# First stage in rounds of one k-tile, and matmul operands at one place modulo 512 bytes

## The chip, the core and the metric

The kernel runs on one core of one Trainium2 chip. The metric is device time in microseconds (us) of one execution; several runs are taken and the median is given. The core's engines are TensorE (PE in the profile; its weight loads stand apart as PEld), VectorE (DVE), ScalarE (ACT), GpSimd (POOL) and SyncE (SP), which here only issues DMAs. Each engine runs its own instructions in order and waits on semaphores for the others.

## What is computed

Two layers of a hybrid encoder on 256 tokens of width 1024, all in float32. Cut to what matters here:

```python
cond = jax.nn.silu(c)
for l in range(2):
    mod = (cond @ ada_w[l] + ada_b[l])[:, None, :]          # 1024 -> 6 x 1024
    sh1, sc1, g1, sh2, sc2, g2 = jnp.split(mod, 6, axis=-1)
    h = rmsnorm(x, norm1_g[l]) * (1 + sc1) + sh1
    proj = h @ w_in[l] + b_in[l]                            # 1024 -> 6733 columns
    ...                                                     # three attention mixers on parts of proj
    x = x + g1 * (y @ w_out[l])                             # y: gated sum of three branch projections
    h = rmsnorm(x, norm2_g[l]) * (1 + sc2) + sh2
    gu = h @ w_ffn_in[l]                                    # 1024 -> 2 x 2816
    x = x + g2 * ((silu(gu[..., :2816]) * gu[..., 2816:]) @ w_ffn_out[l])
return rmsnorm(x, final_g)
```

Almost all of the time goes into the dense products: `w_in`, `w_branch`, `w_out`, `w_ffn_in`, `w_ffn_out`.

## The kernel before, in words

**Splitting.** Each float32 operand of a dense product is split into a high part (rounded to the fp32r type by ScalarE) and a low part (the rest, by a VectorE subtraction). A product is then three matmuls: high·high, high·low, low·high (`mm3`, lines 322 to 324, with the weights' columns as the moving operand; `mm3_T`, lines 466 to 468, with the activations as the moving operand). `block_W` (lines 499 and 500) puts high and low activations side by side: one matmul of 512 columns and one of 256.

**Tiles.** The contraction dimension is cut into k-tiles of 128. The split activations lie in one tile `hT` (high and low, two token halves, eight k-tiles); the feed-forward's hidden activations in `aT0` and `aT1`. Weights arrive by DMA in raw tiles of up to four k-tiles, are split into a pair of tiles `whi` and `wlo` of up to two k-tiles (a piece), and the pieces wait in a pool: six in `splitp`, and a few more in an extra pool that exists in the first stage (`start`, 2), around the output projection (4) and in `ffn_out` (`end0`, `end1`, 3). `new_piece` takes from `splitp` first and from the extra pool when `splitp` is full.

**Places.** Pools are laid out in SBUF one behind the other, in the order in which they are opened, and tiles in a pool likewise, so a tile's address follows from the sizes ahead of it. Counted as bytes past a multiple of 512, in the kernel before: `hT` starts at 256; the pieces of `splitp` at 128; the pieces of the extra pools, `aT0` and `aT1` at 352; the attention outputs `oh` and `ol` at 416 (layer 0) and 480 (layer 1). A block of 128 fp32 columns is 512 bytes, so all slices of `hT`, `aT` and the 512-column weights start at the same remainder as their tile. A block of 456, 326 or 320 columns starts its second k-tile elsewhere.

**The first stage** (`start`, lines 1082 to 1243) works the first four blocks of `w_in` of layer 0 (512, 456, 512 and 512 columns). It needs, for each k-tile, two sums of the adaLN product (`ada_sum`, line 348, on VectorE, which read a raw `ada_w` tile of 1 MB), the modulated and split activations (`modulate`, lines 1144 to 1149), and the split weights (`split`, lines 1159 and 1162). Before, it runs in four rounds of two k-tiles: a raw weight tile `raw0` holds two k-tiles, ten of them are allowed (`START_RAWS`), and a piece holds two k-tiles. In the first round each piece is split in two halves, with the halves of the two k-tiles interleaved. The order of VectorE, ScalarE, TensorE and GpSimd in this stage is the order in which the code is written. The list `plan` sets the order of all loads on SyncE's queue; eight completion lanes are used in turn by the loads of SyncE and ScalarE, so a load waits until the eighth one before it has landed. After the stage the pieces are made by `pump` and taken by `get`.

Of the kernel before, what the change touches and what calls it, by code (L numbers as in the profile page):

```python
# [11 lines left out]
F32 = mybir.dt.float32  # L12
# [6 lines left out]
P = 128  # L19
# [75 lines left out]
def hybrid_encoder(ctx: ExitStack, tc: tile.TileContext, a):  # L95
# [4 lines left out]
    START_BLOCKS, START_RAWS, START_EXTRA = 4, 10, 2  # L100
# [49 lines left out]
    def emit_load(i):  # L150
        it = plan[i]
        if it[0] == "p":
            _, src, off, w = it
            raw = start_pool[0].tile([P, 2 * 512], F32, tag="raw0", name="raw0", bufs=START_RAWS)
            nc.sync.dma_start(raw[:, :2 * w], flat(src, off, [[4 * w, P], [1, 2 * w]]))
            raws[i] = raw
            return
        if it[0] == "w":
            _, src, off, nk, w = it
        else:  # L160
            src, nk, w = a["ada_w"], 4, 512
# [163 lines left out]

    hTT = const.tile([P, 2, T, KT, P], F32R, name="hT")
    hT = [hTT[:, i] for i in range(2)]
# [718 lines left out]
    def start_piece(i, p):  # L1046
        w = len(IN_BLOCKS[i][1])
        return ("p", a["w_in"], IN_OFF[i] + (p // 2) * P * 4 * w + (p % 2) * 2 * w, w)

    ada = ada_items(0, "s1")  # L1050
    for p in range(KT // 2):
        wp = [start_piece(i, p) for i in range(START_BLOCKS)]
        plan += [ada[2 * p], *wp, ada[1]] if p == 0 else [ada[2 * p], *wp[:-1], ada[2 * p + 1], wp[-1]]
# [28 lines left out]
    def start():  # L1082
# [50 lines left out]
        def sums(kt, between=lambda: None):  # L1133
            r = take()
            ada_sum(0, kt, 0, r)
            between()
            ada_sum(0, kt, 1, r)
            free(0)
# [12 lines left out]
        def split(n=1):  # L1151

            w = plan[st_item[0]][3]
            r = take()
            hi, lo = new_piece(2, w)
            cs = [slice(i * 2 * w // n, (i + 1) * 2 * w // n) for i in range(n)]

            def high(i):
                nc.scalar.activation(hi[:, cs[i]], r[:, cs[i]], AF.Copy)

            def low(i):
                nc.vector.tensor_sub(lo[:, cs[i]], r[:, cs[i]], hi[:, cs[i]].bitcast(F32))  # L1162
                if i == n - 1:
                    free(1)

            return high, low
# [5 lines left out]
        def products(i, kt, pc):  # L1172
            k = kt % 2
            if IN_BLOCKS[i][0] in BY_FEATURE:
                for f in range(len(IN_BLOCKS[i][1]) // P):
                    feature_mm(first[i], f, kt, k, pc)
            else:
                for t in range(T):
                    mm3(first[i][t], hT[0][:, t, kt, :], hT[1][:, t, kt, :], pc[0][:, k], pc[1][:, k],
                        start=kt == 0, stop=kt == KT - 1)  # L1180

        for p in range(KT // 2):
            k0 = 2 * p
            if p == 0:
                sums(0)
                parts = [split(2)]
                parts[0][0](0)
                rest = modulate(0, on_act=False)
                parts[0][1](0)
                rest()  # L1190
                for i in range(1, START_BLOCKS):
                    parts.append(split(2))
# [9 lines left out]
                for i, (high, low) in enumerate(parts):  # L1202
                    if i > 1:
                        high(1)
                    low(1)
                    if i == 0:
                        rest()
            else:
                sums(k0)
                high, low = split()  # L1210
                high(0)
                rest = modulate(k0)
                low(0)
                rest()
                for i in range(1, START_BLOCKS):
                    if i == START_BLOCKS - 1:
                        sums(k0 + 1)
                    high, low = split()
                    high(0)
                    if i == START_BLOCKS - 1:  # L1220
                        rest = modulate(k0 + 1)
                    low(0)
            pcs = [ready.pop(0) for _ in range(START_BLOCKS)]
            for i in range(START_BLOCKS):
                products(i, k0, pcs[i])
            if p:
                rest()
            for i in range(START_BLOCKS):
                products(i, k0 + 1, pcs[i])
            got[0] += 4  # L1230
            for pc in pcs:
                piece_out[pc[3]] -= 1
            if p == 0:
# [5 lines left out]
            if p == 1:  # L1239
# [13 lines left out]
    with tc.tile_pool(name="start", bufs=1) as start_pool[0]:  # L1253
        piece_pools[1] = (start_pool[0], START_EXTRA, 4 * START_BLOCKS)
# [89 lines left out]
```

## Time and profile before

| | us |
|---|---|
| median of 3 runs (lowest, highest) | 862.37 (862.35, 864.16) |
| the profiled execution, its own time | 861.53 |
| its span, from the first to the last instruction | 859.8 |
| TensorE busy in the span | 840.1 |
| VectorE busy in the span | 664.4 |
| ScalarE busy in the span | 496.1 |

The span is cut into stretches in one view, and into instructions in order of time in another. A matmul's end is modelled in this profile, and matmuls overlap in their pipeline, so a matmul's price is read from the distance between the starts of two consecutive ones, not from its duration. The granted clock of TensorE is 1.00 (2.4 GHz) in the stretches shown below.

### The profile page before, as it was taken

What the parts mean: (1) busy time and instruction counts of PE and PEld (TensorE: products, weight loads), DVE (VectorE), ACT (ScalarE), POOL (GpSimd) and SP (SyncE); (2) the same over time, 40 slices, a digit from 0 to 9 for tenths busy, and PEclk for the clock granted to TensorE, in tenths of its full rate; (3) what the DMA queues carried; (4) which work ended last, traced back from release to release, by engine and by line L of the source; (5) the groups of instructions that cost most, each with busy time, mean ns of one, the idle gap of its engine ahead of it and who ended that gap; (6) DMA issues with size and microseconds to landing.
All of it is one profiled execution on the core that took longest, in us unless ns stands there. A gap on an engine that the chain in (4) does not pass through costs nothing.

```text
span 859.8 us, 14019 instructions
## 1 busy us (share of the span) xinstructions
PE 840.1 (98%) x5366; PEld 752.3 (87%) x5366; DVE 664.4 (77%) x1148; ACT 496.1 (58%) x874; POOL 73.9 (9%) x131
## 2 busy tenths in 40 slices
PE   6999999999999999999999999999999999999996
PEld 5899898999888888888889999898998888888885
DVE  5996988969896888797475886787998766768734
ACT  6566956764564656564355576767466545556521
POOL 5720210000010000000012013000000100000001
PEclk9999999999999999999999999999999999999998
DMA  9977566669846756599354456387795565546701
GB/s 350 416 263 241 196 218 229 221 245 335 327 151 245 282 215 244 219 342 380 120 195 127 156 189 233 148 282 267 281 373 184 200 223 223 192 150 255 311 23 50
DMA packets 32707, 199.91 MB, mean 233 GB/s; under 512 B 4040, under 2 KB 4304, under 8 KB 14208
## 3 DMA queue, kind: packets, MB, share of 16 engines
q1 hardware_dynamic: 30816, 194.25, 61.1%
q0 software_dynamic: 1232, 4.31, 1.6%
q8 instruction: 42, 0.69, 0.3%
q10 hardware_dynamic: 592, 0.46, 0.2%
q14 instruction: 25, 0.20, 0.1%
HBM read 197.96 MB, written 1.05 MB: 231 GB/s over the span
## 4 chain that ended last, share of the span: by engine, by line
PE 86%; DVE 6%; DMA 3%; issue 2%; ACT 2%; ACTq 0%; POOLq 0%; POOL 0%; DVEq 0%
PE ps_g L499 15%; PE ps_g L322 11%; PE ps_g L324 11%; PE ps_g L323 11%; PE ps_g L500 8%; PE ps_g L466 7%; PE ps_g L467 7%; PE ps_g L468 7%; DVE wlo L196 2%; DMA raw<-in_ada_w_dram 2%; DVE raw L348 2%; PE ps_x L692 1%; PE ps_x L834 1%; PE ps_x L690 1%; PE ps_x L827 1%
## 5 line engine op out<-in xcount | busy, mean ns | idle before, releaser
L196 DVE TENSOR_TENSOR wlo<-raw,whi 128x1024 fp32r<-128x1024 f32 (+5 forms) x284 | 313.1, 1122 | 78.3 <-ACT whi L195 76.2
L195 ACT ACTIVATE whi<-raw 128x1024 fp32r<-128x1024 f32 (+5 forms) x284 | 271.7, 971 | 164.3 <-PE ps_g L324 61.0
L499 PE MATMUL ps_g<-hT,whi 128*128 128x512 f32 x576 | 203.2, 394 | 0.0
L500 PE MATMUL ps_g<-hT,wlo 128*128 128x256 f32 x576 | 162.9, 283 | 0.0
L348 DVE CUSTOM_DVE_ANT_0 raw<-raw,cond,adab 128x1024 f32<-128x1024 f32 x96 | 123.1, 1299 | 24.1 <-DMA raw<-in_ada_w_dram 24.1
L466 PE MATMUL ps_g<-hT,whi 128*128 128x256 f32 x480 | 138.5, 289 | 0.0
L468 PE MATMUL ps_g<-hT,wlo 128*128 128x256 f32 x480 | 135.4, 282 | 0.0
L467 PE MATMUL ps_g<-hT,whi 128*128 128x256 f32 x480 | 135.3, 282 | 0.0
L499 PEld LDWEIGHTS ps_g<-hT,whi 128*128 128x128 f32 x576 | 108.2, 188 | 24.7
L322 PE MATMUL ps_g<-whi,hT 128*128 128x512 f32 (+4 forms) x320 | 118.5, 370 | 1.7 <-ACT hT L1148 1.7
L323 PE MATMUL ps_g<-wlo,hT 128*128 128x512 f32 (+4 forms) x320 | 116.5, 364 | 0.1
L324 PE MATMUL ps_g<-whi,hT 128*128 128x512 f32 (+4 forms) x320 | 116.5, 364 | 0.0
L500 PEld LDWEIGHTS ps_g<-hT,wlo 128*128 128x128 f32 x576 | 108.3, 188 | 0.1
L466 PEld LDWEIGHTS ps_g<-hT,whi 128*128 128x128 f32 x480 | 90.4, 188 | 3.7 <-issue 3.7
L467 PEld LDWEIGHTS ps_g<-hT,whi 128*128 128x128 f32 x480 | 90.5, 189 | 0.3 <-issue 0.3
L468 PEld LDWEIGHTS ps_g<-hT,wlo 128*128 128x128 f32 x480 | 90.4, 188 | 0.3 <-issue 0.3
L322 PEld LDWEIGHTS ps_g<-whi,hT 128*128 128x128 f32 x320 | 60.2, 188 | 11.9 <-ACT hT L1148 2.3
L324 PEld LDWEIGHTS ps_g<-whi,hT 128*128 128x128 f32 x320 | 60.1, 188 | 8.1 <-DVE hT L1149 0.3
L323 PEld LDWEIGHTS ps_g<-wlo,hT 128*128 128x128 f32 x320 | 60.3, 188 | 7.9 <-DVE wlo L1162 0.6
L322 PE MATMUL ps_g<-whi,aT 128*128 128x512 f32 (+1 forms) x176 | 67.0, 381 | 0.0
L323 PE MATMUL ps_g<-wlo,aT 128*128 128x512 f32 (+1 forms) x176 | 66.8, 380 | 0.0
L324 PE MATMUL ps_g<-whi,aT 128*128 128x512 f32 (+1 forms) x176 | 66.7, 379 | 0.0
(226 smaller groups left out, 1175.3 us busy)
## 6 DMA issues: line engine op xcount, KB each, us to landing
raw<-in_ada_w_dram SPq DMA_DIRECT2D x46, 1024.0 KB, 5.4
raw<-in_w_ffn_in_dram SPq DMA_DIRECT2D x40, 1024.0 KB, 4.8
raw<-in_w_in_dram SPq DMA_DIRECT2D x30, 1024.0 KB, 5.5
raw<-in_w_ffn_out_dram SPq DMA_DIRECT2D x20, 1024.0 KB, 5.2
raw<-in_w_branch_dram SPq DMA_DIRECT2D x12, 768.0 KB, 4.7
raw<-in_w_in_dram SPq DMA_DIRECT2D x16, 512.0 KB, 13.3
raw<-in_w_out_dram SPq DMA_DIRECT2D x8, 1024.0 KB, 7.2
raw<-in_w_in_dram SPq DMA_DIRECT2D x8, 768.0 KB, 4.4
```

The source lines that it names most:

```text
L195: nc.scalar.activation(hi, r, AF.Copy)
L196: nc.vector.tensor_sub(lo, r, hi.bitcast(F32))
L322: nc.tensor.matmul(ps, lh, wh, start=start, stop=False)
L323: nc.tensor.matmul(ps, lh, wl, start=False, stop=False)
L324: nc.tensor.matmul(ps, ll, wh, start=False, stop=stop)
L348: nc.vector.tensor_tensor_reduce(out=wj, in0=wj, in1=cond, op0=OP.mult, op1=OP.add, scale=ngain[:, l, int(name[2]) - 1, k:k + 1] if name[: ...
L466: nc.tensor.matmul(ps, wh[:, c], ah, start=first, stop=False, skip_group_check=True)
L467: nc.tensor.matmul(ps, wh[:, c], al, start=False, stop=False, skip_group_check=True)
L468: nc.tensor.matmul(ps, wl[:, c], ah, start=False, stop=stop, skip_group_check=True)
L499: nc.tensor.matmul(ps[f], pc[0][:, k, c], hTT[:, :, :, kt, :], start=kt == 0, stop=False)
L500: nc.tensor.matmul(ps[f][:, :S], pc[1][:, k, c], hT[0][:, :, kt, :], start=False, stop=kt == KT - 1)
L690: nc.tensor.matmul(p[:, 0:P], q[:, 0:P], k[:, 0:P], start=True, stop=True)
```

## The change

1. The first stage runs in eight rounds of one k-tile. A raw weight tile holds one k-tile, so a DMA is half as large, and twenty are allowed (the same room). A piece holds one k-tile. Per round the order is: the two sums, two high splits, the modulation, two low splits, the low part of the activations, the other two blocks' splits; then the products. A piece is given back as soon as its block's products are recorded. In the list of loads each `ada_w` tile is followed by the four weight tiles of its k-tile.
2. Three tiles that nothing uses (`gap0`, 384 bytes; `gap1`, 128 bytes; `gap2`, 288 bytes per partition) move what is allocated behind them. Counted past a multiple of 512 bytes, `hT`, all pieces, `aT0` and `aT1` now start at 128; `oh` and `ol` at 192 (layer 0) and 256 (layer 1).

```diff
-    START_BLOCKS, START_RAWS, START_EXTRA = 4, 10, 2
+    START_BLOCKS, START_RAWS, START_EXTRA = 4, 20, 2
...
-            raw = start_pool[0].tile([P, 2 * 512], F32, tag="raw0", name="raw0", bufs=START_RAWS)
-            nc.sync.dma_start(raw[:, :2 * w], flat(src, off, [[4 * w, P], [1, 2 * w]]))
+            raw = start_pool[0].tile([P, 512], F32, tag="raw0", name="raw0", bufs=START_RAWS)
+            nc.sync.dma_start(raw[:, :w], flat(src, off, [[4 * w, P], [1, w]]))
...
+    const.tile([P, 96], F32, name="gap0")
     hTT = const.tile([P, 2, T, KT, P], F32R, name="hT")
+    const.tile([P, 32], F32, name="gap1")
+    small.tile([P, 72], F32, name="gap2", bufs=1)
...
-    ada = ada_items(0, "s1")
-    for p in range(KT // 2):
-        wp = [start_piece(i, p) for i in range(START_BLOCKS)]
-        plan += [ada[2 * p], *wp, ada[1]] if p == 0 else [ada[2 * p], *wp[:-1], ada[2 * p + 1], wp[-1]]
+    for kt, unit in enumerate(ada_items(0, "s1")):
+        plan += [unit, *(start_piece(i, kt) for i in range(START_BLOCKS))]
...
-        for p in range(KT // 2):
-            k0 = 2 * p
-            if p == 0:
-                sums(0)
-                parts = [split(2)]
-                parts[0][0](0)
+        for kt in range(KT):
+            sums(kt)
+            if kt == 0:
+                low = split()
                 rest = modulate(0, on_act=False)
-                parts[0][1](0)
+                low()
                 rest()
                 for i in range(1, START_BLOCKS):
-                    parts.append(split(2))
-                    high, low = parts[i]
-                    high(0)
+                    low = split()
+                    low()
                     if i < 3:
-                        low(0)
                         to_xT(i - 1, 1, pst[i - 1][1])
-                for high, _ in parts[:2]:
-                    high(1)
-                sums(1, between=lambda: low(0))
-                rest = modulate(1)
...
             else:
-                sums(k0)
-                high, low = split()
-                high(0)
-                rest = modulate(k0)
-                low(0)
+                early = [split() for _ in range(2)]
+                rest = modulate(kt)
+                for low in early:
+                    low()
                 rest()
-                for i in range(1, START_BLOCKS):
-                    if i == START_BLOCKS - 1:
-                        sums(k0 + 1)
-                    high, low = split()
-                    high(0)
-                    if i == START_BLOCKS - 1:
-                        rest = modulate(k0 + 1)
-                    low(0)
+                for _ in range(2, START_BLOCKS):
+                    split()()
             pcs = [ready.pop(0) for _ in range(START_BLOCKS)]
             for i in range(START_BLOCKS):
-                products(i, k0, pcs[i])
-            if p:
-                rest()
-            for i in range(START_BLOCKS):
-                products(i, k0 + 1, pcs[i])
+                products(i, kt, pcs[i])
+                piece_out[pcs[i][3]] -= 1
...
-            if p == 0:
+            if kt == 1:
                 nc.gpsimd.dma_start(posi, a["posT"])
...
-            if p == 1:
+            if kt == 3:
                 rope_sines(*angles)
...
-        piece_pools[1] = (start_pool[0], START_EXTRA, 4 * START_BLOCKS)
+        piece_pools[1] = (start_pool[0], START_EXTRA, KT * START_BLOCKS)
```

VectorE's order in the first two k-tiles, before: `raw_117` to `raw_123` are the raw tiles of the four blocks (k-tiles 0 and 1 in each), the `ISA` rows on `raw` with `cond` are the sums.

```order
L1162 TENSOR_TENSOR wlo<-raw_119,whi 128x456
L1162 TENSOR_TENSOR wlo<-raw_121,whi 128x512
L348 ISA raw,msc_221<-raw,cond,adab,ngain 128x1024
L348 ISA msc_221 128x1
L1162 TENSOR_TENSOR wlo<-raw_123,whi 128x512
L348 ISA raw,msh_223<-raw,cond,adab 128x1024
L348 ISA msh_223 128x1
L1162 TENSOR_TENSOR wlo<-raw_117,whi 128x512
L1149 TENSOR_TENSOR hT<-h_257,hT 128x2x128
```

The same place after: `raw_120` to `raw_126` are the four raw tiles of k-tile 0, `raw_131` to `raw_137` those of k-tile 1.

```order
L1160 TENSOR_TENSOR wlo<-raw_122,whi 128x456
L1160 TENSOR_TENSOR wlo<-raw_124,whi 128x512
L1160 TENSOR_TENSOR wlo<-raw_126,whi 128x512
L352 ISA raw,msc_240<-raw,cond,adab,ngain 128x1024
L352 ISA msc_240 128x1
L352 ISA raw,msh_242<-raw,cond,adab 128x1024
L352 ISA msh_242 128x1
L1160 TENSOR_TENSOR wlo<-raw_131,whi 128x512
L1160 TENSOR_TENSOR wlo<-raw_133,whi 128x456
L1150 TENSOR_TENSOR hT<-h_330,hT 128x2x128
```

The low split of the fourth block of k-tile 0 (`raw_123` before, `raw_126` after) now stands ahead of both sums of k-tile 1 instead of between them.

SyncE's queue behind the two loads of `x`, before; the sizes are partitions by float32 elements:

```order
L166 DMA raw<-in_ada_w_dram 128x1024 x2
L155 DMA raw_117<-in_w_in_dram 128x1024
L155 DMA raw_119<-in_w_in_dram 128x912
L155 DMA raw_121<-in_w_in_dram 128x1024
L155 DMA raw_123<-in_w_in_dram 128x1024
L166 DMA raw<-in_ada_w_dram 128x1024 x2
```

And after:

```order
L166 DMA raw<-in_ada_w_dram 128x1024 x2
L155 DMA raw_120<-in_w_in_dram 128x512
L155 DMA raw_122<-in_w_in_dram 128x456
L155 DMA raw_124<-in_w_in_dram 128x512
L155 DMA raw_126<-in_w_in_dram 128x512
L166 DMA raw<-in_ada_w_dram 128x1024 x2
```

Half as many bytes of weights stand between the first and the second `ada_w` tile.

## Rows read from the trace of the kernel before

**Rows 1.** The page: busy time by engine (part 1), chain by engine (part 4)

```profile
PE 840.1 (98%) x5366; PEld 752.3 (87%) x5366; DVE 664.4 (77%) x1148; ACT 496.1 (58%) x874; POOL 73.9 (9%) x131
...
PE 86%; DVE 6%; DMA 3%; issue 2%; ACT 2%; ACTq 0%; POOLq 0%; POOL 0%; DVEq 0%
```

**Rows 2.** Stretches: us, PE, PEld, DVE, ACT, POOL busy (x), clock, DMA share, GB/s

```profile
0.00:20.00 20.00, 13.50 (x76) 11.74 (x76) 11.55 (x22) 11.48 (x21) 9.84 (x34) 1.00 0.91 345
20.00:40.00 20.00, 17.62 (x110) 15.55 (x111) 18.86 (x27) 12.51 (x20) 17.72 (x24) 1.00 1.02 416
```

**Rows 3.** TensorE in order of time, first stage: start, duration, instruction [idle before]

```profile
11.73 0.51 PE L322 MATMUL ps_g<-whi,hT 128*128 128x512 f32 x1 [0.77 <-ACT hT L1148]
...
17.95 0.39 PE L468 MATMUL ps_x<-hT,wlo 128*128 128x256 f32 x1 [1.64 <-DVE wlo L1162]
...
19.12 0.28 PE L468 MATMUL ps_x<-hT,wlo 128*128 128x256 f32 x1
20.29 0.50 PE L322 MATMUL ps_g<-whi,hT 128*128 128x512 f32 x1 [0.89 <-ACT hT L1148]
...
32.96 0.39 PE L468 MATMUL ps_x<-hT,wlo 128*128 128x256 f32 x1 [1.90 <-DVE wlo L1162]
...
56.16 0.39 PE L322 MATMUL ps_g<-whi,hT 128*128 128x512 f32 x1
...
61.62 0.28 PE L466 MATMUL ps_g<-hT,whi 128*128 128x256 f32 x1
```

**Rows 4.** VectorE in order of time, first stage

```profile
13.35 0.71 DVE L1162 TENSOR_TENSOR wlo<-raw,whi 128x512 fp32r<-128x512 f32 x1 [0.53 <-ACT whi L1159]
15.93 1.35 DVE L348 CUSTOM_DVE_ANT_0 raw<-raw,cond,adab 128x1024 f32<-128x1024 f32 x1 [1.87 <-DMA raw<-in_ada_w_dram]
...
19.01 0.09 DVE L348 DVE_READ_ACCUMULATOR2_ANT msh<- 128x1 f32 x1
...
21.79 0.68 DVE L1162 TENSOR_TENSOR wlo<-raw,whi 128x512 fp32r<-128x512 f32 x1
22.39 1.33 DVE L348 CUSTOM_DVE_ANT_0 raw<-raw,cond,adab 128x1024 f32<-128x1024 f32 x1
...
44.07 1.34 DVE L348 CUSTOM_DVE_ANT_0 raw<-raw,cond,adab 128x1024 f32<-128x1024 f32 x1
...
46.54 1.22 DVE L1162 TENSOR_TENSOR wlo<-raw,whi 128x1024 fp32r<-128x1024 f32 x1
```

**Rows 5.** TensorE in ffn_out of layer 0: pieces of extra pool, then others

```profile
398.62 0.39 PE L324 MATMUL ps_g<-whi,aT 128*128 128x512 f32 x1
...
400.66 0.39 PE L324 MATMUL ps_g<-whi,aT 128*128 128x512 f32 x1
...
403.65 0.39 PE L322 MATMUL ps_g<-whi,aT 128*128 128x512 f32 x1
...
405.28 0.40 PE L323 MATMUL ps_g<-wlo,aT 128*128 128x512 f32 x1
```

**Rows 6.** TensorE at 256-column products: a feature block, then a joint block

```profile
198.75 0.28 PE L467 MATMUL ps_g<-hT,whi 128*128 128x256 f32 x1
...
199.70 0.28 PE L466 MATMUL ps_g<-hT,whi 128*128 128x256 f32 x1
...
299.85 0.40 PE L499 MATMUL ps_g<-hT,whi 128*128 128x512 f32 x1
...
301.26 0.39 PE L499 MATMUL ps_g<-hT,whi 128*128 128x512 f32 x1
```

**Rows 7.** TensorE groups with shapes kept apart: busy, mean of one

```profile
L499 PE MATMUL ps_g<-hT,whi 128*128 128x512 f32 x576 | 203.2, 394 | 0.0
...
L466 PE MATMUL ps_g<-hT,whi 128*128 128x256 f32 x480 | 138.5, 289 | 0.0
...
L322 PE MATMUL ps_g<-whi,hT 128*128 128x512 f32 x160 | 63.8, 399 | 1.7 <-ACT hT L1148 1.7
...
L322 PE MATMUL ps_g<-whi,aT 128*128 128x512 f32 x154 | 60.8, 395 | 0.0
```

More of the change, by code (lines that the diff above doesn't have):

```diff
@@ L1042, in ffn_units, with start_piece @@
         return ws
-    def start_piece(i, p):
+    def start_piece(i, kt):
         w = len(IN_BLOCKS[i][1])
-        return ("p", a["w_in"], IN_OFF[i] + (p // 2) * P * 4 * w + (p % 2) * 2 * w, w)
-    ada = ada_items(0, "s1")
-    for p in range(KT // 2):
-        wp = [start_piece(i, p) for i in range(START_BLOCKS)]
-        plan += [ada[2 * p], *wp, ada[1]] if p == 0 else [ada[2 * p], *wp[:-1], ada[2 * p + 1], wp[-1]]
+        return ("p", a["w_in"], IN_OFF[i] + (kt // 4) * P * 4 * w + (kt % 4) * w, w)
+    for kt, unit in enumerate(ada_items(0, "s1")):
+        plan += [unit, *(start_piece(i, kt) for i in range(START_BLOCKS))]
     plan += mix(mixer_units(0)[2 * START_BLOCKS:], ada_items(0, "g1", "s2"), SKIP0)
@@ L1131, in free, with sums @@
             more_loads()
-        def sums(kt, between=lambda: None):
+        def sums(kt):
             r = take()
-            ada_sum(0, kt, 0, r)
-            between()
-            ada_sum(0, kt, 1, r)
+            for j in range(2):
+                ada_sum(0, kt, j, r)
             free(0)
@@ L1149, in modulate, with split, low @@
             return lambda: nc.vector.tensor_sub(hT[1][:, :, kt, :], h, hT[0][:, :, kt, :].bitcast(F32))
-        def split(n=1):
+        def split():
             w = plan[st_item[0]][3]
             r = take()
[L1155 to L1166, printed above, removed]
+            hi, lo = new_piece(1, w)
+            nc.scalar.activation(hi, r[:, :w], AF.Copy)
+            def low():
+                nc.vector.tensor_sub(lo, r[:, :w], hi.bitcast(F32))
+                free(1)
+            return low
         first = [[(ps_gemm if i < 2 else lambda w: ps_x()[:, :w])(min(512, len(IN_BLOCKS[i][1]))) for _ in range(T)]
@@ L1172, in products @@
         def products(i, kt, pc):
-            k = kt % 2
             if IN_BLOCKS[i][0] in BY_FEATURE:
                 for f in range(len(IN_BLOCKS[i][1]) // P):
-                    feature_mm(first[i], f, kt, k, pc)
+                    feature_mm(first[i], f, kt, 0, pc)
             else:
                 for t in range(T):
-                    mm3(first[i][t], hT[0][:, t, kt, :], hT[1][:, t, kt, :], pc[0][:, k], pc[1][:, k],
+                    mm3(first[i][t], hT[0][:, t, kt, :], hT[1][:, t, kt, :], pc[0][:, 0], pc[1][:, 0],
@@ L1195, in start @@
                     if i < 3:
-                        low(0)
                         to_xT(i - 1, 1, pst[i - 1][1])
-                for high, _ in parts[:2]:
-                    high(1)
-                sums(1, between=lambda: low(0))
-                rest = modulate(1)
[L1202 to L1206, printed above, removed]
-                        rest()
-            else:
-                sums(k0)
-                high, low = split()
-                high(0)
-                rest = modulate(k0)
-                low(0)
-                rest()
-                for i in range(1, START_BLOCKS):
-                    if i == START_BLOCKS - 1:
-                        sums(k0 + 1)
-                    high, low = split()
-                    high(0)
-                    if i == START_BLOCKS - 1:
-                        rest = modulate(k0 + 1)
-                    low(0)
+            else:
+                early = [split() for _ in range(2)]
+                rest = modulate(kt)
+                for low in early:
+                    low()
+                rest()
+                for _ in range(2, START_BLOCKS):
+                    split()()
@@ L1223, in start @@
             pcs = [ready.pop(0) for _ in range(START_BLOCKS)]
             for i in range(START_BLOCKS):
-                products(i, k0, pcs[i])
-            if p:
-                rest()
-            for i in range(START_BLOCKS):
-                products(i, k0 + 1, pcs[i])
+                products(i, kt, pcs[i])
+                piece_out[pcs[i][3]] -= 1
             got[0] += 4
-            for pc in pcs:
-                piece_out[pc[3]] -= 1
-            if p == 0:
+            if kt == 1:
```

## Prediction

> **What bounds the kernel now.** I read the busy times first, then the chain of waits, then the first stage in order of time, and last the distances between matmul starts. TensorE is busy 98% of the span and makes up 86% of the chain that ended last; VectorE is 6% of it, DMA 3%, issue and ScalarE 2% each [rows 1]. So a gain must either close one of the few holes on TensorE or shorten its matmuls.
>
> The holes are in the first stage. Its products start at 11.73 us and the first matmul of the next block starts at 61.62 [rows 3]. The last round's second k-tile, without a hole, takes from 56.16 to 61.62, 5.46 us; eight of these are 43.7 us, and the stage took 49.9. Of the 6.2 us lost, three holes of 1.64, 0.89 and 1.90 us are marked; the rest is slow restarts. The first hole waits for the low split of the fourth block, which stands behind a sum on VectorE, and that sum waited 1.87 us for the second `ada_w` tile [rows 4]. The second hole waits for the activations of k-tile 1, made from the same sums. The third is a low split again, behind the sums of another k-tile.
>
> The rest of the time is matmuls back to back, and there the distance between starts differs with the place of the operands. In `ffn_out`, nine steps from 398.62 to 400.66 take 2.04 us, 226.7 ns each; seven steps from 403.65 to 405.28 take 1.63 us, 232.9 ns each [rows 5]. These are the same instructions on the same activations. The first pieces are of the extra pool and, like `aT`, start at 352 past a multiple of 512 bytes; the second are of `splitp`, at 128. So operands at one place are 6.2 ns (2.7%) faster per matmul of 512 columns. Of 256 columns the trace has no run at one place. Eight steps of a feature block (`hT` at 256, pieces at 128) take 0.95 us, 118.8 ns each; four pairs of 512 and 256 columns take 1.41 us, 352.5 ns a pair [rows 6].
>
> **The first stage, step by step.** Half of each of the four weight tiles, 996 KiB or 1.02 MB together, no longer stands ahead of the second `ada_w` tile. At 345 GB/s, the mean of the first 20 us [rows 2], that is 3.0 us: the sum that started at 15.93 has its data from about 13.0. VectorE's third low split ends at 14.06 [rows 4]; the fourth now follows without a sum between, and ends at about 15.0 (ScalarE's high split of it, queued behind a copy, is done near 14.4). So the sums of k-tile 1 start at 15.0 and take 2.47 us (44.07 to 46.54). From the end of the sums to the first matmul that uses them it was 19.10 to 20.29, 1.19 us, so k-tile 1 starts on TensorE at 18.7. K-tile 0 ends without its hole near 17.5. The first hole goes; the second stays with about 1.2 us.
>
> From there VectorE's round counts: sums 2.47; three low splits of 512 columns at 0.60 (21.79 to 22.39); by the same rate estimates of 0.55 for 456 columns and 0.34 for 256; 0.2 of waiting for ScalarE, whose modulation and third high split (about 1.6 us) outlast two low splits and the activations' low part (1.5). That is 5.36 us against 5.46 on TensorE, so VectorE stays just ahead. The sums of k-tile 7 start at 15.0 + 6 x 5.36 = 47.2, its products at 47.2 + 2.47 + 1.19 = 50.9, and they end at 56.3: 5.3 us sooner than 61.62. Pieces are eight either way, now two rounds of products instead of four; each is given back block by block, and the splits for round n+2 come after round n, so this adds no wait. GpSimd computes the angles beside it and is slowed by VectorE; its result is due after k-tile 3. I take 0.3 off for that: **-5.0 us**.
>
> SyncE's queue gets sixteen more loads, each half as large, and all of them pass the eight lanes. Eight consecutive loads still hold about 3 MB. A round needs 1024 + 996 KiB, 2.07 MB: 4.97 us at the 416 GB/s of the second stretch, 6.0 us at 345 [rows 2]. Which of these half-size loads reach, no row shows. At 6.0 the sums of k-tile 7 wait until about 50.4, the products end at 59.5 and the gain is 2.1 us. So this term lies between -2.1 and -5.5.
>
> **The places.** All products with `hT` or `aT` get both operands at 128. Counts are from the groups [rows 7]: the `mm3` form with 512 columns is three times 160 + 154, 942 matmuls, of which 137 have one place already as laid out. In short runs the faster distance is not reached at once, so I take 5.0 ns instead of 6.2 for 805: -4.0 us. Narrower `mm3` products, 360 of them at one place after the change, at the same 5.0: -1.8. The 576 pairs of `block_W`: if each matmul saves 6.2 a pair saves 12.4; I take 5.0 a pair: -2.9. The feature blocks, 480 + 64 per line and three lines, 1632 matmuls of 256 columns: I take half of 6.2, 3.0 ns: -4.9. For these last two the ends are far apart. The good end is 6.2 per matmul whatever its width, if what is saved belongs to the weight load beside it. The bad end is 1.7 ns lost per matmul, since 352.5 less 232 leaves about 120.5 for the 256 columns of the pair, the slowest such distance here. Values near the middle, as no row decides. `oh` and `ol` move from 288 or 352 to 64 or 128 behind the pieces: nothing either way.
>
> In sum -13.6. About 1.0 of it lies in the first stage, where VectorE's 5.36 us would then bound, and a tenth is taken off where TensorE is not what the chain follows: 0.9 x 12.6 = **-11.3 us**. Bounds: -24 with 6.2 everywhere, +4 with the bad end and nothing from the 512-column form.
>
> Rows 5 show the same instruction at 226.7 and 232.9 ns. The Trainium skill (page "SBUF — State Buffer", section "Who interferes with whom") says that TensorE has independent read ports for the moving operand and the weight load and never waits on anyone; by it the places would change nothing, and the sum would be the first stage alone (the third rival). This case's trace disagrees by 6.2 ns for 512 columns; for 256 it has nothing at one place.
>
> For the half-size loads the rows give 345 to 416 GB/s over both sizes. The Trainium skill (the same page, section "The DMA setup-cost knee") advises the largest transfers, since each pays a fixed cost of some 2 us; it speaks against halving them, and its fit would lower the rate of a transfer alone. With several in flight I go by the rows.
>
> **The sum.** -5.0 - 11.3 = -16.3 from the profiled execution's 861.5 gives 845.2. The median before, 862.4, is 0.8 above that execution, so I predict **846 us** (its own range 841 to 852).
>
> **Rivals.**
> - The saving belongs to the weight load, whatever the width. For: a load of the same 128 weight columns goes with each matmul. Against: the 256-column distances lie only 1.8 ns apart. The good end, -24 x 0.9 - 5 with the first stage's share off: about 837.
> - A second engine takes over: VectorE is busy 77%, and half the gain of the places becomes waits for splits: 862.4 - 5.0 - 5.7 = 852. Against: TensorE is busy 98% [rows 1], so splits are seldom late now.
> - The places do nothing outside the runs shown: 857. Rows 5 speak against it, as they alternate within one stage.
> - The loads run at 345 GB/s and the first stage gives 2.1: 849.
> - Both of the last two: 860.3, within what counts as no change.
> - Slower: one place is the bad place for 256 columns. There are 1632 + 576 such matmuls; what else is gained is about 5 + 5.2 us, so it decides from 4.6 ns each, 123.4 instead of 118.8. At 6.2 ns the other way: 13.7 - 10.2, 866. Against: the slowest 256-column distance in rows 6 is about 120.5.
>
> **How the numbers follow.** Likeliest 0.40; weight load 0.18; second engine 0.12; places nothing 0.10; slow loads 0.08; both 0.06; bad place 0.06. Faster by over 0.2% (1.7 us, about what can be told from no change) are the first five, 0.88; same 0.06; slower 0.06. The range 837 to 858 leaves out the last two and a part of the second.
>
> **What would show it.** First stage: the fourth low split of k-tile 0 right behind the third, the second `ada_w` sum at about 15 instead of 15.93, one hole near 17.5 to 18.7 and none near 31, the next block's first matmul near 56. If holes before each k-tile wait for `ada_w`, the loads were mis-sized. Places: 227 ns per 512-column matmul throughout `ffn_out` and the output projections; feature blocks at 115.8, `block_W` pairs at 347. If they stay at 118.8 and 352.5 that term was wrong; if TensorE's gaps grow behind `whi` and `wlo`, the second engine was.

## The result and the profile after

Over six executions each on the same chip, the changed kernel takes 855.62 us in the median (854.55 to 857.85) and the kernel before 861.85 (859.91 to 864.16). The ratio is 0.9932, with a 95% interval of 0.9918 to 0.9947: by the ratio a gain of 5.9 us, between 4.6 and 7.1. I had predicted 846, a gain of 16. The change helps, by little more than a third of what I worked out.

The profiled execution after is the longest of its six (857.85 us, span 856.1). Its page, busy time and chain by engine, against [rows 1]:

```profile
PE 837.3 (98%) x5366; PEld 752.8 (88%) x5366; DVE 666.7 (78%) x1160; ACT 497.7 (58%) x886; POOL 73.3 (9%) x131
...
PE 76%; DVE 10%; DMA 7%; issue 3%; ACT 2%; POOL 1%; ACTq 0%; POOLq 0%; DVEq 0%; SPq 0%
```

TensorE is still busy 98% of the span. Its share of the chain is 76% here, where it was 86%; but a second profile of the same kernel, further down, has 83%, and the kernel with places alone 73%. The share moves that much between executions, so I read nothing from it. The first two stretches, columns as in [rows 2], and then a finer cut with TensorE alone:

```profile
0.00:20.00 20.00, 12.78 (x77) 11.19 (x77) 12.33 (x24) 11.65 (x22) 8.83 (x29) 1.00 0.88 318
20.00:40.00 20.00, 20.00 (x117) 18.20 (x118) 18.69 (x32) 11.95 (x25) 17.89 (x29) 0.91 1.03 404
...
20.00:22.00 2.00, 2.00 (x6) 0.64 1.04 405
22.00:24.00 2.00, 2.00 (x6) 0.50 1.05 424
```

Two things are new. In the first 20 us the DMAs move 318 GB/s, not 345. And the granted clock, 1.00 in the whole first stage before, is 0.50 from 22 to 24 us: TensorE runs at 1.2 GHz there. TensorE in order of time, first stage, against [rows 3]:

```profile
12.35 0.49 PE L322 MATMUL ps_g<-whi,hT 128*128 128x512 f32 x1 [1.55 <-ACT hT L1149]
...
17.86 0.28 PE L472 MATMUL ps_x<-hT,wlo 128*128 128x256 f32 x1
19.92 0.50 PE L322 MATMUL ps_g<-whi,hT 128*128 128x512 f32 x1 [1.78 <-ACT hT L1149]
...
20.86 0.63 PE L322 MATMUL ps_g<-whi,hT 128*128 128x512 f32 x1
21.29 0.63 PE L323 MATMUL ps_g<-wlo,hT 128*128 128x512 f32 x1
...
55.06 0.50 PE L322 MATMUL ps_g<-whi,hT 128*128 128x512 f32 x1 [0.41 <-ACT hT L1149]
...
60.68 0.28 PE L470 MATMUL ps_g<-hT,whi 128*128 128x256 f32 x1
```

The holes inside a round are gone, one of 1.78 us stands between k-tiles 0 and 1, and right behind it 512 columns take 0.43 us from start to start, twice the usual. The next block starts at 60.68 instead of 61.62. (This execution is unlucky in both; the experiments show others.) The operand places, in the stages of [rows 5] and [rows 6]:

```profile
400.80 0.39 PE L324 MATMUL ps_g<-whi,aT 128*128 128x512 f32 x1
...
402.84 0.39 PE L324 MATMUL ps_g<-whi,aT 128*128 128x512 f32 x1
...
195.76 0.28 PE L470 MATMUL ps_g<-hT,whi 128*128 128x256 f32 x1
...
196.72 0.28 PE L472 MATMUL ps_g<-hT,wlo 128*128 128x256 f32 x1
...
295.81 0.40 PE L503 MATMUL ps_g<-hT,whi 128*128 128x512 f32 x1
...
297.22 0.40 PE L503 MATMUL ps_g<-hT,whi 128*128 128x512 f32 x1
```

Nine steps of 512 columns, on pieces of `splitp`, take 2.04 us, 226.7 ns each, as hoped (232.9 before). Eight steps of a feature block take 0.96 us, 120.0 ns each, where it was 118.8: slower. Four pairs take 1.41 us, 352.5 a pair: no change. For all back-to-back matmuls of a form, the mean distance from start to start (from the trace; counts are of the distances used):

```
                                  before   after   places   rounds   192 bytes
                                                   alone    alone    (below)
512 columns, weights moving  925   232.4   227.5   227.6    232.4    228.4
384 columns, weights moving  174   175.9   174.2   174.2    175.9    173.3
320; 326                   90 each 146.7; 150.3 before, 146.5; 150.6 after
256 columns, weights moving  131   117.2   119.0   119.0    117.2    119.0
256 columns, hT moving      1547   118.7   119.7   119.7    118.7    116.3
pair: 512                    569   230.6   233.9   233.8    230.6    234.9
      256                    569   120.5   116.6   116.6    120.5    118.3
```

Two different kernels with the same places agree to 0.1 ns, so these distances follow the places alone. Counted together, before to after: -4.5 us for 512 columns, -0.3 for 384, +0.2 for 256 with weights moving, +1.5 for the feature products, -0.3 for the pairs. That is -3.4 us where the prediction had -13.6.

### The profile page after: what moved, and what is told of

The parts are those of the page before. It is cut to its first block, busy times and chain, and to the rows that moved or that the text cites. A ratio compares the mean times of both kernels' runs of the same rounds, so it can differ in the third digit from the quotient of the medians.

```text
span 856.1 us, 14107 instructions
## 1 busy us (share of the span) xinstructions
PE 837.3 (98%) x5366; PEld 752.8 (88%) x5366; DVE 666.7 (78%) x1160; ACT 497.7 (58%) x886; POOL 73.3 (9%) x131
## 4 chain that ended last, share of the span: by engine, by line
PE 76%; DVE 10%; DMA 7%; issue 3%; ACT 2%; POOL 1%; ACTq 0%; POOLq 0%; DVEq 0%; SPq 0%
PE ps_g L503 16%; PE ps_g L322 8%; PE ps_g L324 8%; PE ps_g L323 8%; PE ps_g L504 8%; PE ps_g L470 7%; PE ps_g L472 7%; PE ps_g L471 7%; DVE wlo L196 4%; DMA raw<-in_ada_w_dram 3%; DMA raw<-in_w_in_dram 3%; PE ps_x L838 1%; PE ps_x L696 1%; DVE raw L352 1%; PE ps_x L831 1%
```

## The experiments

The ratios are against the kernel before on the same chip. The first two kernels each do one half of the change.

**Places alone.** The kernel before with the three spacing tiles.

```diff
+    const.tile([P, 96], F32, name="gap0")
     hTT = const.tile([P, 2, T, KT, P], F32R, name="hT")
+    const.tile([P, 32], F32, name="gap1")
+    small.tile([P, 72], F32, name="gap2", bufs=1)
```

> The kernel before with the three spacing tiles alone: operand places as in the changed kernel, the first stage as before. Theory A, that the trace of the changed kernel shows what places are worth: from start to start of successive matmuls, 805 products of 512 columns of a weight piece go from 233 to 227.5 ns (-4.2 us), the block_W pairs from 351.1 to 350.5 ns (576 pairs, -0.3), the 256-column feature products from 118.7 to 119.7 ns (1,574, +1.6), the narrower pieces by -0.2: -3.1 us, so -2.5 to -4 against the kernel before, and the same distances in this run. Theory B, my forecast: every form gains, -13.6 us. Theory C, places are worth nothing and all came from the first stage: within 1 us of the kernel before.

Measured: 859.05 against 861.36, ratio 0.9977 (0.9963 to 0.9991): -2.0 us (-0.8 to -3.2). The distances are those of theory A, as the table above has them; the time falls a little short of its 2.5 to 4, which the interval reaches. Theory B falls. Theory C's 1 us touches the edge of the interval in time; the distances speak against it.

**Rounds alone.** The changed kernel without those three tiles.

> The changed kernel without the three spacing tiles: rounds over one k-tile, operand places as in the kernel before. Theory A, the parts add up: -6.2 + 3.1 = about -3 us against the kernel before, with one hole of 1.6 to 1.9 us before k-tile 1, and the next block's first matmul 1 to 3.5 us sooner than at 61.62 us. Theory B, my forecast: -5.0 us from the first stage, next block's first matmul near 56 us. Theory C, that the first stage gives nothing: within 1 us of the kernel before.

Measured: 859.38 against 861.36, ratio 0.9980 (0.9967 to 0.9993): -1.7 us (-0.6 to -2.8). TensorE in order of time at the first hole, at two later k-tiles and at the next block, then VectorE where the second `ada_w` sum stands, where a later one waits and at the last one, and ScalarE at the last activations:

```profile
17.35 0.28 PE L469 MATMUL ps_x<-hT,wlo 128*128 128x256 f32 x1
18.70 0.50 PE L322 MATMUL ps_g<-whi,hT 128*128 128x512 f32 x1 [1.07 <-ACT hT L1146]
...
35.88 0.50 PE L322 MATMUL ps_g<-whi,hT 128*128 128x512 f32 x1
...
52.49 0.39 PE L322 MATMUL ps_g<-whi,hT 128*128 128x512 f32 x1
...
57.97 0.28 PE L467 MATMUL ps_g<-hT,whi 128*128 128x256 f32 x1
...
14.95 1.34 DVE L349 CUSTOM_DVE_ANT_0 raw<-raw,cond,adab 128x1024 f32<-128x1024 f32 x1
...
26.32 1.34 DVE L349 CUSTOM_DVE_ANT_0 raw<-raw,cond,adab 128x1024 f32<-128x1024 f32 x1 [0.36 <-DMA raw<-in_ada_w_dram]
...
48.46 1.34 DVE L349 CUSTOM_DVE_ANT_0 raw<-raw,cond,adab 128x1024 f32<-128x1024 f32 x1
...
51.69 0.42 ACT L1146 ACTIVATE hT<-h 128x256 fp32r<-128x256 f32 x1
```

In time that is less than theory A's -3, and the interval touches theory C's 1 us. In the profile the first stage is the one that I had forecast, up to k-tile 1: the sum starts at 14.95 (forecast 15.0), and the hole lies at 17.63 to 18.70 (forecast 17.5 to 18.7). The next block starts 3.65 us sooner than before, not 5.0. And of 3.65 us only 1.5 are left at the end of the span (858.3 against 859.8). Most of the rest goes behind 126 us, as TensorE and VectorE in order of time show:

```profile
126.34 0.28 PE L468 MATMUL ps_g<-hT,whi 128*128 128x256 f32 x1
128.87 0.29 PE L784 MATMUL ps_x<-ident,F 128*128 128x128 f32 x1 [2.25 <-DVE lg L787]
...
125.64 1.28 DVE L349 CUSTOM_DVE_ANT_0 raw<-raw,cond,adab 128x1024 f32<-128x1024 f32 x1 [2.30 <-DMA raw<-in_ada_w_dram]
```

and in stretches (TensorE's busy time, then clock, DMA share, GB/s):

```profile
128.00:130.00 2.00, 1.13 (x7) 0.81 0.00 0
130.00:132.00 2.00, 2.00 (x13) 0.50 0.03 8
132.00:134.00 2.00, 2.00 (x16) 0.84 0.00 0
```

The kernel before, at the same instruction and in the stretches behind it:

```profile
132.30 0.40 PE L783 MATMUL ps_x<-ident,F 128*128 128x128 f32 x2 [2.05 <-DVE lg L786]
```

```profile
132.00:134.00 2.00, 1.70 (x14) 1.00 0.00 0
134.00:136.00 2.00, 2.00 (x17) 1.00 0.04 8
```

TensorE waits there for VectorE's bias tiles, and VectorE has waited 2.30 us for an `ada_w` tile. The idle stretch, 2.25 us, is only 0.2 longer than before; but then TensorE runs at 1.2 GHz for about 3.4 us, which the kernel before did not in its profile. That costs 1.4 us: from the first matmul behind the stretch to the 1,000th it takes 22.43 us here, and with the full clock 21.09 in the kernel before and 21.02 to 21.03 in the six other profiles without 192 bytes. By the 1,000th matmul the lead is 2.1 us.

**The two small loads.** In the changed kernel's profile SyncE issues the second `ada_w` load only at 8.47 us, when `norm_gT` has landed. Test: put `ada_bT` and `norm_gT` on another queue.

```diff
-        nc.scalar.dma_start(adab, a["ada_bT"])
-        nc.scalar.dma_start(ngain, a["norm_gT"])
+        nc.gpsimd.dma_start(adab, a["ada_bT"])
+        nc.gpsimd.dma_start(ngain, a["norm_gT"])
```

> The changed kernel with the two small loads of ada_bT and norm_gT on the GpSimd queue in place of ScalarE's. Theory A, that the second ada_w load is held at its issue (8.47 us) by the completion of norm_gT, and the transfer rate sags to 203 and 267 GB/s behind that: it is issued by 7 us, the second ada_w sum starts before 15.2 us (15.75 now), the hole before k-tile 1 shrinks to under 1.2 us (1.78 to 1.94 now), and the time falls by 0.5 to 2 us below the changed kernel's. Theory B, that the hole is set by the loads' rate alone or by the chain on ScalarE and VectorE behind them: within 0.4 us of the changed kernel. Theory C: the two small loads land later by GpSimd's queue, the seeds' scaling moves behind 8.6 us, and the first product with it: slower by up to 1 us.

Measured: 856.37, ratio 0.9940 (0.9924 to 0.9957), the same as the changed kernel's 0.9932 within the intervals. Theory A's signs are in the profile: the load is issued at 4.84 us, the second sum starts at 15.02, and the hole is 1.09 us. But the kernel with rounds alone, which issued the load at 7.99, has 14.95 and 1.07, and in both the sum follows the fourth low split without waiting for its tile. So I see no gain from the early issue: theory A's saving isn't seen, and B is the nearer, though the interval doesn't rule out C. The late landing of `norm_gT` explains why the changed kernel's profiled execution was slow to start: VectorE waited 1.21 us for it ahead of the sums, and the first product came at 12.35 (11.5 to 12.1 in all but one of the others).

**A probe for the places.** Back-to-back matmuls on one tile of zeros.

> Another program: back-to-back matmuls on zeros, which leaves out the whole computation. Three forms (512 contiguous columns; 256 columns in two parts; a pair of 512 in four parts and 256 in two), each at 16 places of the moving operand 32 bytes apart with the weights' place held, then the weights' place moved in steps of 64 bytes with the moving operand held, then both moved together. Theory A, that only the distance of the places modulo 512 bytes counts: moving the weights mirrors moving the operand, moving both changes nothing; 227 ns at distance 0 and 233 elsewhere for 512 columns, as in the kernels. Theory B, that the absolute place of one operand counts: one of the two single moves changes nothing. Theory C, that the places do not count and something else of the two kernels does: all rows alike within 0.5 ns. For the 256-column form the kernels show 118.7 ns at distance 128 and 119.7 at 0, so its best place is expected away from 0; for the pair 351.1 and 350.5.

One group is one case of 24 equal matmuls. Rows of its trace in order of time: 512 columns with the moving operand 0, 32 and 256 bytes behind the weights; 256 columns at 0 and 192 bytes; and 256 columns with the weights moved by 64 bytes instead:

```profile
30.96 5.38 PE L115 MATMUL ps_g<-arena 128*128 128x512 f32 x23
...
36.41 5.53 PE L115 MATMUL ps_g<-arena 128*128 128x512 f32 x23
...
75.54 5.40 PE L115 MATMUL ps_g<-arena 128*128 128x512 f32 x23
...
202.55 3.04 PE L115 MATMUL ps_g<-arena 128*128 128x256 f32 x24
...
219.62 2.89 PE L115 MATMUL ps_g<-arena 128*128 128x256 f32 x24
...
247.82 2.90 PE L115 MATMUL ps_g<-arena 128*128 128x256 f32 x24
```

Less the modelled length of the last one (0.39 and 0.28 us), a step is 5.38 - 0.39 over 22, 226.8 ns; then 233.6 and 227.7; 120.0; 113.5; 113.9. Start to start, over the moving operand's distance in bytes:

```
                       0      32     64     96     128    160    192    224    256
512 columns          226.7  233.4  228.9  233.9  233.5  234.0  233.3  233.1  227.2
256 columns          120.0  117.9  117.8  119.6  118.8  117.5  113.4  118.1  119.8
pair 512 + 256       354.1  346.7  351.8  350.5  351.0  346.9  352.9  353.1  354.1
```

Up to 480 bytes the rows repeat within about 1 ns: the period is 256 bytes, not 512. Moving the weights mirrors it to about 1 ns (512 columns, weights at 64: 233.5, at 192: 229.0; 256 columns, weights at 64: 113.6). Moving both leaves 226.9 to 228.5, 119.6 to 119.7 and 346.5 to 347.1, whatever the place. So theory A holds with half the period, except for the pair at 0, which has two values. Distance 0 is the best for 512 columns and the worst for 256, whose best is 192. The pair at 0 came at 346.5 in one part of the program and at 353 to 354 in others.

**The place that the probe ranks best for the feature products.** `hT` 192 bytes behind the pieces, modulo 256, in the changed kernel and alone in the kernel before.

```diff
-    const.tile([P, 96], F32, name="gap0")
+    const.tile([P, 16], F32, name="gap0")
-    const.tile([P, 32], F32, name="gap1")
-    small.tile([P, 72], F32, name="gap2", bufs=1)
+    const.tile([P, 48], F32, name="gap1")
+    small.tile([P, 8], F32, name="gap2", bufs=1)
```

> The changed kernel with other spacing: hT 192 bytes behind the pieces' place modulo 256 (the changed kernel has 0), everything else at equal places modulo 256. Theory A, that the distance of the two operands' places modulo 256 bytes sets the pace, as the probe has it: feature products of 256 columns from 119.7 to 113.5 ns (1,574: -9.8 us), 805 products of 512 columns from 227.5 to 228.9 (+1.1), 576 pairs from 350.5 to 352.9 (+1.4): -7.3 us against the changed kernel, so about 848. Theory B, that the kernel, with DMA and other engines at SBUF beside it, shows only part of what the empty machine shows (there 120.0 to 113.4): -2 to -4, about 852. Theory C, my forecast's idea that equal places modulo 512 are best for every form: slower than the changed kernel by 10 us or more (865).

> The kernel before with that same spacing alone. Theory A: against the kernel before, feature products 118.7 to 113.5 ns (-8.2 us), 512 columns 233 to 228.9 (-3.3), pairs 351.1 to 352.9 (+1.0): -10.5, about 851. Theory B: -4 to -6, about 856. Theory C: no better than the kernel before, 861.

Measured: 856.78, ratio 0.9941 (0.9919 to 0.9964), in the changed kernel, and 860.70, ratio 0.9979 (0.9967 to 0.9991), in the kernel before. Neither differs from the first spacing beyond the intervals. The last column of the first table says why: feature products fall to 116.3 ns, not 113.5, and pairs and 512 columns pay 2.7 and 0.9 for it. The 116.3 is a mean of two paces: of some 1,575 distances in the changed kernel with 192 bytes, about 60% are 117 to 119 ns and 35% 113 or 114. By the distances that would still be some 3 us below the first spacing; from the start of the 1,000th to that of the 4,200th matmul it is 0.9 to 1.4 (480.9 and 481.1 us, where the first spacing takes 482.1 to 482.3), and in the time nothing is to be told. So even theory B asked for too much, and where the rest goes stays open. Theory C's idea, that equal places are best for every form, falls too: in the changed kernel unequal ones cost nothing that can be measured.

**A second probe**, with finer steps.

> Back-to-back matmuls on zeros again, the whole computation left out. The three forms with the resident operand (hT's part) from 160 to 256 bytes behind the pieces' place in steps of 8 bytes, then 384 and 320 columns and 256 contiguous columns in steps of 32, then the pair at 0, 192, 0, 128, 0, 192, 256, 0 in turn. Theory A, that only the distance modulo 256 counts: 0 and 256 agree, 192 repeats the first probe's 228.9, 113.4 and 352.9, and there is one best place for each form; the 384 columns follow the 512, the contiguous 256 follow the 256 in parts. For the pair at 0, where the first probe had 354.1, 353.0 and 346.5 at one distance, theory A1 says that it depends on the place in the program (the same 0 gives both), theory A2 that the predecessor's place sets it.

Measured: 512 columns 228.9 at 192, as before, and 227.1 at 256; in between, steps of 8 bytes lie from 228.2 to 233.3. 256 columns in two parts come at 117.8 at 192 this time, and at 120.6 to 124.8 at the odd multiples of 8 bytes (168, 184 and so on). The same 256 columns in one part are at 113.4 at 192. 384 columns take 173.3 to 176.7, 320 columns 146.4 to 146.7 everywhere. The pair at 0, tried four times, was 346.7 behind another form, 352.8 behind a pair at 192, 353.1 behind 128 and 353.0 behind 256. Theory A2 isn't borne out by the last, which stood behind its own place modulo 256; one distance has two paces, and what chooses between them stays open. Theory A holds for the 512 columns and for the pair at 192, and falls otherwise: 384 columns don't follow the 512 (173.3 at 32, 96 and 192 too), and 256 in parts don't repeat 113.4. For that form the probes differ in the order of the three products of a round: in the second two moving operands follow on one block of weights and then the other block comes, as in the kernel's `mm3_T`; the first has another order. So the 113.4 that theory A of the 192 bytes was priced with isn't the only pace there, and both paces come without any DMA beside them, which theory B had as the reason.

**The idle stretch near 127 us.** What do the stretch and the lower clock behind it cost? The later `ada_w` units of layer 0 go three pieces later in the list of loads, so that VectorE has no such sum ahead of the bias tiles; as a control, the same in the kernel before; and the changed kernel once more.

```diff
-    SKIP0, SKIP1 = 14, 22
+    SKIP0, SKIP1 = 17, 22
```

> The changed kernel with the first layer's later ada_w units three pieces later in the load list (SKIP0 17 for 14), which takes the ada_w sum that waits 2.20 us for its load out of VectorE's row ahead of the bias tiles for which TensorE stands still 2.0 to 2.3 us near 127 us. Theory A, that the first stage's gain is given back as one stretch at 1.2 GHz behind an idle stretch of TensorE (in this or in the first stage, by where the idle time falls): the idle stretch near 127 us shrinks under 1 us, the clock stays at full speed through 126 to 136 us, and the time falls by 2.0 us for the stretch and by up to 1.4 us more for the clock: 852 to 853.5. Theory B, that the clock has no part in it: -2.0 us or less against the changed kernel (853.5 to 855), and the same as with the kernel before. Theory C: the later units only move the wait to another place: no change.

> The kernel before with that same edit, as the control. Its profile has the same idle stretch (129.97 to 132.30 us) with the clock at full speed behind it. Theory A: -2.0 us for the stretch alone, so 859 to 860. Theory B: the same gain as in the changed kernel. Theory C: no change.

> The changed kernel itself once more, for a comparison on the same chip with the two kernels above, and for a second profile. Theory A: 855 to 856.5 in the median; if the profile has the first stage as the kernel with rounds alone had it (first product at 11.9, hole before k-tile 1 of 1.35 us, next block at 58.0 us), then the lower clock shows near 128 to 134 us instead of 20 to 24 us, or nowhere (then its span is under 853.5). Theory B: no such exchange.

```
                        SKIP0 14            SKIP0 17
kernel before           862.01              859.88  ratio 0.9979 (0.9966 to 0.9993)
changed kernel          856.51, 0.9927      853.16  ratio 0.9896 (0.9877 to 0.9915)
                        (0.9907 to 0.9948)
```

The edit is worth 2.1 us in the kernel before and 3.3 in the changed one (1.8 and 2.7 by the ratios). So most of it is the idle stretch itself, which the kernel before has as well. The surplus of about 1 is what theory A asks for, but it lies within these intervals, so the medians alone don't rule B out. The profiles speak for A: in the six where TensorE is idle there for at most 0.53 us, the full clock follows; of the six with 1.76 to 2.75 us, three have the lower one. The changed kernel with SKIP0 17, TensorE at the same instruction in order of time, and the stretch behind it:

```profile
127.03 0.40 PE L787 MATMUL ps_x<-ident,F 128*128 128x128 f32 x2 [0.23 <-DVE lg L790]
```

```profile
128.00:132.00 4.00, 4.00 (x34) 1.00 0.02 4
```

The changed kernel once more, the same two views; this execution is one of the two shortest of its six (854.11 us), and without the edit VectorE waited 1.57 us for the `ada_w` tile, TensorE 0.40 for VectorE:

```profile
127.72 0.41 PE L787 MATMUL ps_x<-ident,F 128*128 128x128 f32 x2 [0.40 <-DVE lg L790]
```

```profile
128.00:132.00 4.00, 4.00 (x34) 1.00 0.01 4
```

Neither has the lower clock here. Their next blocks start at 57.97 and 58.48, and of these 3.65 and 3.1 us nothing is given back: by the 1,000th matmul they lead by 5.3 and 4.6, since the kernel before has its own idle stretch in between, and at the end of the span by 8.8 and 7.4.

**Further kernels.** Both SKIP0 17 and the two small loads on GpSimd; and SKIP0 17 with the 192 bytes.

> The changed kernel with both: the two small loads on GpSimd's queue and the ada_w units three pieces later. Theory A: next block's first matmul at 58.0 us in the profile, no idle stretch over 1 us near 127 us, full clock there, time 851.5 to 853.5 us. Theory B (small loads worth nothing beside the later units): the same as with the later units alone, within 0.5 us.

> The changed kernel with the ada_w units three pieces later and hT 192 bytes behind the pieces modulo 256. Theory A, that of the two spacings the traces rank the 192 bytes first by a little (from the 1,000th to the 4,200th product 481.5 to 481.8 us against 482.0 to 482.7 at 0 and 484.0 to 484.9 before): 0.5 to 1.5 us below the kernel with the later units alone, 852 to 852.7 us. Theory B, that the gain of the feature products (119.7 to 116.2 ns) is offset by pairs and 512 columns and by waits elsewhere: within 0.5 us of it, 852.7 to 853.7.

Measured: 853.80 (ratio 0.9904, 0.9886 to 0.9922) and 853.25 (0.9896, 0.9874 to 0.9919). Theory B is the nearer for both (the second ran on another chip; its ratio is that of SKIP0 17 alone): neither can be told from SKIP0 17 alone. The 1,000th to the 4,200th matmul take 480.0 us in the second's profile and 481.6 in that of SKIP0 17 alone, start to start (the figures in its expectation are 0.4 to 0.7 above those that I give); that lead is lost elsewhere (its next block starts only at 60.01). So the changed kernel with SKIP0 17 is the version to keep: 853.16 us, 8.9 below the kernel before and 3.3 below the changed kernel on the same chip.

## Why the prediction was wrong, point by point

**Places: wrong in three terms out of four.** "805 at 5.0" was right: -4.0 us forecast, -4.5 measured. The steps that failed are those where I carried the saving of the 512-column form over to forms of which no run stood at one place. Narrower products: -1.8 forecast, -0.1 measured; 384 columns gain 1.7 ns, 320 and 326 nothing, 256 lose 1.8. Pairs: -2.9 forecast, -0.3 measured; the 512 part loses 3.3 ns, the 256 part gains 3.9. Feature products: -4.9 forecast with half the saving, +1.5 measured; each loses 1.0 ns. The rival of the bad place had the sign right, and its price of 6.2 ns far too high. I had rows of 256 columns at distance 128 alone and took a middle between two ends, which was a guess; neither end was measured on that form at one place.

The page "SBUF — State Buffer" of the Trainium skill (section "Who interferes with whom") gives TensorE independent read ports for the moving operand and for the weight load, and has it wait for nobody. The traces disagree in a program that does nothing else: 234.0 or 226.7 ns, and 120.0 or 113.4, by the distance of the two operands alone.

Of the -3.4 us, how much reaches the end? From the 1,000th to the 4,200th matmul the three profiles with the places of before take 483.6 to 484.5 us, the six with the changed ones 481.6 to 482.3: -2.1 in this part, which is what its distances add up to. The kernel with places alone gains 2.0 us in all (0.8 to 3.2).

**First stage: right up to k-tile 1, then too large by 1.4 to 1.9 us.** In six of the eight profiles with the rounds the next block starts at 57.97 to 58.48; that is 3.1 to 3.65 us sooner than at 61.62, where I said 5.0 (near 56). In the other two the first product came late (12.35 and 12.59). The sum at 15.0 and the hole at 17.5 to 18.7 came as worked out. The step that failed is the pace from there on. I let VectorE's round of 5.36 us set the end, though by my own numbers TensorE's k-tile, 5.46, is the longer: seven of them from 18.7 end at 56.9, not at 56.3. The kernel with rounds alone shows this: the activations of the last k-tile are ready at 52.11 (51.69 + 0.42), 3.65 us behind the start of its sums, as forecast, but TensorE is busy with the k-tile ahead until 52.49, and its last three k-tiles take 5.48 to 5.49 us each. The four ahead of them take 5.61 to 5.85. Two of these are late through VectorE, whose rounds there took 5.87 (0.36 of waiting for an `ada_w` tile) and 5.85 (0.40 for the angles, near the 0.3 that I took off); the others took 5.41 to 5.50.

**What the prediction left out.** The sum was taken as if all that TensorE saves early stays saved. The kernel before has an idle stretch of 2.05 us at 130 us in its profile, which I did not list, since it lies behind the first stage. It moves along with the earlier start, as the `ada_w` load that it hangs on does, and gives back only 0.2 us. But a stretch at 1.2 GHz behind it takes 1.4 us more, and one behind the hole at 18 us about as much: the changed kernel takes 40.8 us from k-tile 1 to the next block in its first profile and 39.6 in its second. In the old first stage it costs next to nothing (41.3 to 41.4 us there, with it or without). The profiles have that lower clock at 20 to 24 us in the changed kernel, places alone, 192 bytes alone and the kernel before with SKIP0 17 (granted clock 0.52 to 0.60 there), and at 128 to 136 in rounds alone, the small loads and, again, 192 bytes alone (0.60 to 0.66). Six have it in neither, the kernel before and the changed kernel's second profile among them. So it isn't the change alone that brings it. It is a price that a profile without it does not show.

Together: -2.0 to -3.4 for the places, -3.1 to -3.65 for the first stage, and 0 to 1.6 given back, is -3.5 to -7; measured -5.9. By their ratios the two halves alone gain 2.0 and 1.7 us, 3.7 together, and why the whole gains 2.2 more stays open. Of the rivals, "places do nothing outside the runs shown", 857, is nearest in time, but the places do change the 512-column and the feature products, with opposite signs. "A second engine takes over" (852) isn't borne out: TensorE's distances alone account for the small gain of the places. The measured time lies in the range of 837 to 858 and outside the 841 to 852 of the likeliest, so the wide range held it and the mechanism did not.

## What to carry to other kernels

A saving measured on one shape of instruction is not a price for its neighbours: where the trace has no run of the other shape, measure it by itself before counting on thousands of them. A probe of a few hundred microseconds showed here what no reading of the trace could; it holds for the order of products that it ran, and the kernel's order had a second pace. And an early gain has to be followed to the next places where TensorE waits: what stands behind them (here a lower clock in some executions, 1.4 us) can take part of it. Closing such a wait can pay by itself: one number gained 2.1 us in the kernel before and 3.3 in the changed one.

## What the runs showed of the hardware

- The pace of back-to-back fp32r matmuls depends on the distance, modulo 256 bytes, of the moving operand from the weights that are loaded beside it. 512 columns: 226.7 ns at 0, 228.9 at 64, 233 to 234 at the other multiples of 32. 256 columns: 113.4 at 192, 117.5 to 118.8 mostly, 119.6 to 120.0 at 0 and 96. 320 columns: no effect (146.4 to 146.7).
- The best of both forms is 0.443 ns a column (226.7 / 512, 113.4 / 256).
- One distance can have two paces: the pair at 0 at 346.5 or at 353, 256 columns in two parts at 192 at 113.4 or 117.8. In the kernels the mean lies between (350.5 and 116.3).
- Idle stretches of TensorE of 1.5 to 2.6 us are followed by about 3.4 us at 1.2 GHz in some executions (6.8 us once), and stretches of 1.6 to 2.75 us by the full clock in others (2.05 us in the kernel before: full clock; 1.78 and 2.25 us: 1.2 GHz). So their length alone doesn't decide it here. The page "TensorE: Matmul & The Clock Gate" of the Trainium skill ("What's actually happening") has just these two levels, and lets activity release the lower one; the 0.50 of these stretches agrees with the levels.
